# Regrouping the stages of attention, and seven by-7 steps in the second half of the down product

## The chip, the cores and the metric

The kernel runs on one core of one Trainium2 chip. The metric is the device time of one execution in microseconds (us). Before the change it is 1697.8 us, the median of three runs (1697.61 to 1697.96).

The engines are called PE (matrix products), PEld (its weight loads), DVE (vector), ACT (scalar, activations), POOL and SP (which here mostly issues DMA transfers).

## The reference

One decoder block on 256 tokens of width 2048, all in float32:

```python
a    = rmsnorm(h, norm_mix_pre)
proj = a @ w_in                      # q,k,v of 3x8 attention heads, 4 recurrence parts, 2 gates
# attention: per head three groups (window, dilation) = (128,1), (512,4), (2048,16),
#   rotary q and k, outputs mixed by their softmax denominators  -> attn (256 x 1024)
# recurrence: S_t = diag(f_t) S_{t-1} + k_t v_t^T, o_t = S_t^T q_t, per-head norm, swish gate
#   -> r_out (256 x 1024)
y = sigmoid(gate_a) * (attn @ w_attn_branch) + sigmoid(gate_r) * (r_out @ w_hgrn_branch)
h = h + rmsnorm(y @ w_mix_out, norm_mix_post)
gt, up = split(rmsnorm(h, norm_ffn_pre) @ w_ffn_gate_up)
h = h + rmsnorm((silu(gt) * up) @ w_ffn_down, norm_ffn_post)    # inner width 5632
```

The three attention groups are done as one softmax over 512 scores per query: the denominators that mix them are then those of the joint softmax.

## The kernel before

**Products.** Every large product is done in a reduced-precision format of PE with both operands split into a high and a low half (ACT rounds the high half, DVE subtracts it to get the low half). One block product is then three matmuls: high x high, high x low, low x high. Each matmul has a 128x128 stationary operand and up to 512 columns of the other. The small products of attention and recurrence, and the transposes (products with an identity matrix), are done in plain float32.

**Items.** The main loop goes over a list of items. An item is either a *chunk* of a narrow block (kind "W" and "N": 4 or 2 rows of 128 of the weight matrix) or a *step* of a wide block (256 rows, two groups of 512 columns, both halves of the tokens). A plain step is 8 block products, 24 matmuls. A *by-7* step gets the same result from 7 block products, 21 matmuls, out of sums of weight pieces and sums of activation pieces: `split_wide` makes the weight sums on DVE (lines 434, 440, 441) and splits them, and `seven_sums` (lines 522 to 529) makes and splits the activation sums. For item i the loop first calls `prepare(i)`, which splits the weights of item i+2 (tiles `w` and `wl`; for a by-7 step also `dh` and `dl`, the raw weights' halves) and starts loads further ahead. Then `multiply(i)` issues the matmuls into the PSUM banks `acc` or `aux`. Then `advance(evacs)` issues one part of a finished block's evacuation, and `advance_lanes()` advances each of the two lanes by one stage.

**Lanes.** A lane holds generators; each `yield` in one ends its stage for this item. The recurrence of four heads (`recurrence(half)`) runs in lane 0. It has six levels, three items each: products `q,kk` in the first item, DVE work on `at`, `kk`, `q` and `end` in the second, nothing in the third. A queue holds the attention of 2 x 4 heads (line 913); a free lane takes the next head. A head has two parities `par`, and each of these has the scores (3 products, `aux<-qk,qk`), the masked maximum on DVE (line 917), exponential and sum on ACT (line 921), reciprocal and scaling on DVE (lines 923, 924), four transposes on PE (line 930), their copy on ACT (line 933) and four products with the values (`aux<-pt,v`). Their items, counted from the scores, are 0, 1, 1, 2, 4, 5 and 6, and the next parity's scores are in item 7. After the second parity's values one more item writes the result's high half (ACT, line 943) and low half (DVE, line 944). So PE does something for one parity in items 0, 4 and 6.

The order in each engine's queue is the order in which this loop issues; nothing reorders it afterwards. Tiles of one tag share a fixed number of buffers: three `w` slots, so the split of item i+2 waits until PE has read the weights of item i-1; four `aux` banks; sixteen slots `r` of 128x1024 floats that hold, in the down product, the activations `act` loaded from DRAM, their halves `a`, the activation sums `so` and the gains `fpost`.

**Down product.** The last two wide blocks multiply the inner activations with `w_ffn_down`, each with 22 steps (m = 0 to 21) and 1024 output columns. `DOWN` (line 47) names the by-7 steps: 4, 7, 10, 13, 16, 19 in the first half and 3, 6, 9, 12, 15, 18 in the second. `prep_act` (line 1397) loads, splits and, for a by-7 step, sums the activations of a step; the sums of step m are kept under `a7[m]`, and so the two halves compute theirs separately. While the second half begins, DVE and ACT still evacuate the first (`down_sum` line 1425, `down_square` line 1429, `down_gain` line 1434, tile `fz`).

Of the kernel before, what the change touches and what calls it, by code (L numbers as in the profile page):

```python
# [17 lines left out]
AF = mybir.ActivationFunctionType  # L18
OP = mybir.AluOpType

P = 128
S = 256
# [3 lines left out]
KF = FF // P  # L26
# [17 lines left out]
GATE_UP3 = [(3, 0), (4, 0), (0, 2), (5, 0), (1, 1), (6, 0), (2, 2), (7, 0)]  # L44
GATE_UP4 = [(4, 0), (5, 0), (0, 2), (6, 0), (1, 1), (2, 2), (3, 1), (7, 0)]
PLACE = (0, 2, 1, 3)
DOWN = [[(m, m in by7) for m in range(KF // 2)] for by7 in (range(4, 20, 3), range(3, 19, 3))]

N_F, N_RAW, N_SPLIT, AHEAD, WARM, BRIDGE = 15, 3, 3, 2, 8, 6

# [50 lines left out]
def tile_hybrid_block(ctx: ExitStack, tc: tile.TileContext, t, out):  # L101
    nc = tc.nc
# [22 lines left out]
    def aux():  # L125
        return auxp.tile([P, 512], F32, tag="aux", name=nm("aux"))
# [7 lines left out]
    def small(s, n=8, bufs=6):  # L134
        return cpool.tile([P, n], F32, tag=f"small{n}", bufs=bufs, name=nm(s))

    def mm(ps, lhsT, rhs, start, stop):
        nc.tensor.matmul(ps, lhsT, rhs, start=start, stop=stop, skip_group_check=True)  # L138
# [66 lines left out]
    def ptile(s):  # L205
        pool, n = (wide_pool[-1], 2) if wide_pool else (fp[0], 5)
        return pool.tile([P, 512], F32, tag="p", bufs=n, name=nm(s))
# [344 lines left out]
    class Split:  # L552
# [20 lines left out]
        def high(self, n, src):  # L573
            nc.scalar.activation(self.slots[n][:, :, 0, :], src, AF.Copy)
# [84 lines left out]
    def flush(q):  # L659
        while q:  # L660
            advance(q)

    def advance_lanes():
        for lane in lanes:
            if not lane and queue:
                lane.append(queue.popleft())
            advance(lane)

    def flush_lanes():
# [201 lines left out]
    qkT, vN = {}, {}  # L871
# [28 lines left out]

    attnT, recT = [], []

    def attention(half, h):
        o = None
        for par in range(2):
            own = slice(par * P, (par + 1) * P)
            ps = aux()
            for g in range(3):
                q, k = qkT["q", half, g], qkT["k", half, g]
                if g == 0:  # L910
                    mm(ps[:, :S], q[:, h, own], k[:, h, :], True, True)
                else:
                    mm(ps[:, P * (g + 1) : P * (g + 2)], q[:, h, own], k[:, h, own], True, True)
            yield
            p = ptile("p")
            m = small("m")
            nc.vector.tensor_tensor_reduce(
                out=p, in0=ps, in1=amask[:, par, :], scale=1.0, scalar=3e38,
                op0=OP.add, op1=OP.min, accum_out=m[:, 0:1],
            )  # L920
            nc.scalar.activation(p, p, AF.Exp, scale=-1.0, bias=m[:, 0:1], accum_out=m[:, 1:2])
            yield
            nc.vector.reciprocal(m[:, 2:3], m[:, 1:2])
            nc.vector.tensor_scalar(p, p, m[:, 2:3], None, op0=OP.mult)
            yield
            yield
            ps = aux()
            for c in range(4):
                cols = slice(c * P, (c + 1) * P)
                nc.tensor.transpose(ps[:, cols], p[:, cols], ident)  # L930
            yield
            pt = ptile("pt")
            nc.scalar.activation(pt, ps, AF.Copy)
            yield
            if o is None:
                o = aux()
            for c in range(4):
                v = vN[half, max(c - 1, 0)][:, c if c < 2 else par, h * P : (h + 1) * P]
                mm(o[:, own], v, pt[:, c * P : (c + 1) * P], c == 0, c == 3)
            yield  # L940
        hi, lo, _ = attnT[0](4 * half + h)
        ov = o[:, :S].rearrange("p (two j) -> p two j", two=2)
        nc.scalar.activation(hi.rearrange("p (j two) -> p two j", two=2), ov, AF.Copy)
        nc.vector.tensor_sub(
            lo.rearrange("p (j two) -> p two j", two=2), ov,
            attnT[0].f32(4 * half + h).rearrange("p (j two) -> p two j", two=2),
        )
        yield


    def recurrence(half):
# [25 lines left out]
        def added(c):  # L977
            ps = aux()
            for n in range(2):
                mm(ps, onesr, hl[c][n], n == 0, n == 1)  # L980
            return ps
# [31 lines left out]
        for lev, w in enumerate(LEVELS):  # L1013
            rows = P - w if w > 8 else P
            ps = aux() if w > 1 else added(0)
            for e in range(8) if w > 1 else ():
                es = slice(e * P, (e + 1) * P)
                mm(
                    spans(ps[:rows, e * 64 : (e + 1) * 64], w), kk[:, e * P : e * P + rows],
                    spans(q[:, es], 2 * w)[:, :, w:], True, True,  # L1020
                )
            yield
            if w < 32:
                nc.vector.copy_predicated(
                    at[:rows].rearrange("p (e n w) -> p e n w", e=8, w=2 * w)[:, :, :, w:],
                    lmask[:rows, lev, :].rearrange("p (n w) -> p n w", w=w)[:, None, :, :]
                    .to_broadcast([rows, 8, 64 // w, w]).bitcast(I32),
                    ps[:rows].rearrange("p (e n w) -> p e n w", e=8, w=w),
                )
# [12 lines left out]
            used += n  # L1042
            nc.vector.tensor_mul(new, end[:, :, 0], end[:, :, 1])
            end = new
            if w == 8 and half == 0:
                nc.scalar.preload_act_table_set("natural_log_exp_and_others")
            yield
            yield
# [352 lines left out]
    def prep_act(m, by7):  # L1401

        q = prepared[0] // 2
        prepared[0] += 1
        fetch_act(q + (m % 2 and 2))
        f = act_in[q][:, m % 2 * 2 : m % 2 * 2 + 2, :]
        x = parts_of[m] = Split("a", 2)
        x.high(0, f)
        yield
        x.low(0, f)  # L1410
        if by7:
            dst = rslot("so").rearrange("p (z n t) -> p z n t", z=2, n=4)
            high, low = seven_sums(f, dst)
            high()
            a7[m] = sums_of(dst)
            yield
            low()
# [74 lines left out]

    def start_attention(half):
        def go():
            queue.extend(attention(half, h) for h in range(4))
        return go

    def begin_branches():
# [202 lines left out]
```

## Time and profile before

| | |
|---|---|
| median of three runs | 1697.8 us |
| the profiled execution | 1698.13 us |
| its span, first to last instruction | 1696.3 us |
| mean granted PE clock | 0.998 |
| instructions | 21711 |

In the rows that follow, `L138` is the line of the one matmul helper, so most PE rows carry it and have to be told apart by their tiles. A row of the timeline gives start, duration, engine, line, operation, result and operands, shape, count, and in brackets the idle time just ahead of it with what ended it. [...] A row of the chain of waits gives start, duration, engine, tile, line and count of the instructions merged into one piece. A row of the waits gives who waited for whom, with total, times and longest.

### The profile page before, as it was taken

What the parts mean: (1) busy time and instruction counts of PE and PEld (TensorE: products, weight loads), DVE (VectorE), ACT (ScalarE), POOL (GpSimd) and SP (SyncE); (2) the same over time, 40 slices, a digit from 0 to 9 for tenths busy, and PEclk for the clock granted to TensorE, in tenths of its full rate; (3) what the DMA queues carried; (4) which work ended last, traced back from release to release, by engine and by line L of the source; (5) the groups of instructions that cost most, each with busy time, mean ns of one, the idle gap of its engine ahead of it and who ended that gap; (6) DMA issues with size and microseconds to landing.
All of it is one profiled execution on the core that took longest, in us unless ns stands there. A gap on an engine that the chain in (4) does not pass through costs nothing.

```text
span 1696.3 us, 21711 instructions
## 1 busy us (share of the span) xinstructions
PE 1685.2 (99%) x8260; PEld 1416.7 (84%) x8260; DVE 1436.2 (85%) x1662; ACT 914.7 (54%) x1034; POOL 3.9 (0%) x13
## 2 busy tenths in 40 slices
PE   9999999999999999999999999999999999999997
PEld 7888888888888888888888888888888888888886
DVE  6999888867998988885668888888888888898997
ACT  6655555544444434445445547555555555565663
POOL 0000000000000000000000000000000000000000
PEclk9999999999999999999999999999999999999999
DMA  8667666768677767787858646777777777777773
GB/s 285 205 224 243 230 233 228 234 222 309 225 254 252 256 223 243 253 310 275 295 172 275 210 162 227 269 250 252 254 255 253 249 248 272 257 266 256 248 244 130
DMA packets 228904, 413.48 MB, mean 244 GB/s; under 512 B 12816, under 2 KB 79552, under 8 KB 226240
## 3 DMA queue, kind: packets, MB, share of 16 engines
q1 hardware_dynamic: 218544, 373.93, 65.4%
q10 hardware_dynamic: 10192, 38.15, 6.0%
q8 instruction: 64, 1.05, 0.3%
q14 instruction: 40, 0.33, 0.1%
q0 software_dynamic: 64, 0.02, 0.0%
HBM read 376.92 MB, written 35.13 MB: 243 GB/s over the span
## 4 chain that ended last, share of the span: by engine, by line
PE 98%; DVE 1%; ACT 0%; issue 0%; DVEq 0%; ACTq 0%
PE acc L138 62%; PE aux L138 34%; PE aux L930 0%; DVE wl L420 0%; PE aux L610 0%; PE aux L1348 0%; DVE fz L1475 0%; PE acc L1348 0%; ACT w L418 0%; ACT junk L1429 0%; PE aux L597 0%; DVE e L1425 0%; PE aux L1110 0%; DVE yT L578 0%; PE aux L1220 0%
## 5 line engine op out<-in xcount | busy, mean ns | idle before, releaser
L138 PE MATMUL acc<-xT,w 128*128 128x256 f32 (+1 forms) x2048 | 366.8, 338 | 0.0
L420 DVE TENSOR_TENSOR wl<-raw,w 128x2048 fp32r<-128x2048 f32 (+1 forms) x141 | 306.6, 2182 | 68.8 <-ACT w L418 67.1
L138 PEld LDWEIGHTS acc<-xT,w 128*128 128x128 f32 x2048 | 311.9, 188 | 44.7 <-DVE w L365 0.3
L418 ACT ACTIVATE w<-raw 128x2048 fp32r<-128x2048 f32 (+1 forms) x141 | 256.3, 1827 | 109.3 <-PE acc L138 35.1
L364 ACT ACTIVATE w<-raw 128x1024 fp32r<-128x1024 f32 x176 | 185.7, 1058 | 220.5 <-PE acc L138 169.6
L365 DVE TENSOR_TENSOR w<-raw,w 128x1024 fp32r<-128x1024 f32 x176 | 214.8, 1221 | 95.9 <-ACT w L364 95.2
L138 PE MATMUL acc<-w,xT 128*128 128x512 f32 x578 | 169.1, 392 | 0.0
L439 ACT ACTIVATE w<-sum 128x1024 fp32r<-128x1024 f32 x56 | 59.5, 1063 | 177.8 <-DVE sum L434 170.6
L138 PE MATMUL acc<-w,hT 128*128 128x512 f32 x472 | 152.7, 391 | 0.4 <-DVE hT L1232 0.4
L447 DVE TENSOR_TENSOR wl<-sum,w 128x1024 fp32r<-128x1024 f32 x112 | 134.8, 1221 | 13.2 <-ACT w L439 13.2
L138 PEld LDWEIGHTS acc<-w,xT 128*128 128x128 f32 x578 | 108.1, 188 | 22.2
L138 PE MATMUL aux<-w,hT 128*128 128x512 f32 x374 | 120.0, 389 | 0.0
L449 DVE TENSOR_TENSOR dl<-raw,dh 128x1536 fp32r<-128x1536 f32 x56 | 98.3, 1756 | 14.3 <-ACT dh L445 12.2
L138 PE MATMUL aux<-w,xT 128*128 128x512 f32 x344 | 109.8, 389 | 0.0
L138 PEld LDWEIGHTS acc<-w,hT 128*128 128x128 f32 x472 | 88.5, 188 | 19.0 <-DVE hT L1232 0.8
L138 PE MATMUL acc<-wl,hT 128*128 128x512 f32 x236 | 91.9, 389 | 0.0
L445 ACT ACTIVATE dh<-raw 128x1536 fp32r<-128x1536 f32 x56 | 82.7, 1476 | 8.0 <-PE aux L138 4.4
L138 PE MATMUL acc<-w,a 128*128 128x512 f32 x268 | 83.7, 389 | 0.0
L138 PE MATMUL aux<-w,a 128*128 128x512 f32 x268 | 83.7, 389 | 0.0
L138 PEld LDWEIGHTS aux<-w,hT 128*128 128x128 f32 x374 | 70.2, 188 | 14.6
L138 PE MATMUL acc<-w,so 128*128 128x512 f32 x234 | 78.8, 391 | 0.0
L138 PEld LDWEIGHTS aux<-w,xT 128*128 128x128 f32 x344 | 64.6, 188 | 13.4
(298 smaller groups left out, 2964.3 us busy)
## 6 DMA issues: line engine op xcount, KB each, us to landing
raw<-in_w_in SPq DMA_DIRECT2D x270, 512.0 KB, 4.8
raw<-in_w_ffn_gate_up SPq DMA_DIRECT2D x156, 512.0 KB, 4.8
raw<-in_w_ffn_down SPq DMA_DIRECT2D x88, 512.0 KB, 5.4
pre<-in_w_ffn_gate_up SPq DMA_DIRECT2D x40, 512.0 KB, 6.5
presum<-pre ACTq DMA_DIRECT2D x20, 1024.0 KB, 4.7
s<-presum SPq DMA_DIRECT2D x40, 512.0 KB, 7.0
raw<-in_w_mix_out SPq DMA_DIRECT2D x32, 512.0 KB, 4.9
act<-acts SPq DMA_DIRECT2D x22, 512.0 KB, 6.5
```

What stands on the lines that cost most here:

```text
L138: nc.tensor.matmul(ps, lhsT, rhs, start=start, stop=stop, skip_group_check=True)
L364: nc.scalar.activation(wh, raw, AF.Copy)
L365: nc.vector.tensor_sub(wl, raw, wh.bitcast(F32))
L418: nc.scalar.activation(hi[:, c], raw[:, c], AF.Copy)
L420: nc.vector.tensor_sub(lo[:, c], raw[:, c], hi[:, c].bitcast(F32))
L439: nc.scalar.activation(hi[:, :1024], s[:, :1024], AF.Copy)
L445: nc.scalar.activation(dhi, d, AF.Copy)
L447: nc.vector.tensor_sub(lo[:, c], s[:, c], hi[:, c].bitcast(F32))
L449: nc.vector.tensor_sub(dlo, d, dhi.bitcast(F32))
```

## The change

Two things are changed.

**Attention.** A lane now takes one generator that works through the queue of heads without leaving it. Within a parity the stages are: scores in item 0, maximum and exponential in item 1, scaling in item 2, transposes in item 3, copy in item 4, nothing in item 5, products with the values in item 6. The next parity's or next head's scores stand in that same item 6, just behind the products with the values. The result's high half is written in the next item just ahead of the maximum, its low half just behind the exponential. A generator that starts while lane 0 is busy puts its first scores off until an item in which the recurrence has issued a level's products (`beat`), three items at the most.

**Down product.** The second half has by-7 steps 2, 4, 7, 10, 13, 16 and 18, seven instead of six. Five of these (4, 7, 10, 13, 16) are by-7 steps of the first half too; their activation sums are kept from there (`m not in a7`) and not made again, which holds five of the sixteen `r` slots from one half to the other.

```diff
-DOWN = [[(m, m in by7) for m in range(KF // 2)] for by7 in (range(4, 20, 3), range(3, 19, 3))]
+DOWN = [[(m, m in by7) for m in range(KF // 2)] for by7 in (range(4, 20, 3), (2, 4, 7, 10, 13, 16, 18))]
...
+    tick, beat = [0], [0]
+
     def advance_lanes():
+        tick[0] += 1
         for lane in lanes:
             if not lane and queue:
-                lane.append(queue.popleft())
+                lane.append(attention())
             advance(lane)
...
-    def attention(half, h):
-        o = None
-        for par in range(2):
+    def attention():
+        done = []
+        for _ in range(3):
+            if not lanes[0] or tick[0] == beat[0]:
+                break
+            yield
+        while queue:
+            half, h = queue.popleft()
+            o = None
+            for par in range(2):
...
                 yield
+                for part in done[:1]:
+                    part()
                 p = ptile("p")
...
                 nc.scalar.activation(p, p, AF.Exp, scale=-1.0, bias=m[:, 0:1], accum_out=m[:, 1:2])
+                for part in done[1:]:
+                    part()
+                done = []
                 yield
...
                 nc.vector.tensor_scalar(p, p, m[:, 2:3], None, op0=OP.mult)
-            yield
-            yield
+                for _ in range(1):
+                    yield
                 ps = aux()
...
                 nc.scalar.activation(pt, ps, AF.Copy)
-            yield
+                for _ in range(2):
+                    yield
                 if o is None:
                     o = aux()
...
                     mm(o[:, own], v, pt[:, c * P : (c + 1) * P], c == 0, c == 3)
-            yield
-        hi, lo, _ = attnT[0](4 * half + h)
...
+            done = attended(4 * half + h, o)
+        yield
+        for part in done:
+            part()
+        yield
+
+    def attended(k, o):
...
+        return [high, low]
...
             ps = aux() if w > 1 else added(0)
+            beat[0] = tick[0]
...
-        if by7:
+        if by7 and m not in a7:
             dst = rslot("so").rearrange("p (z n t) -> p z n t", z=2, n=4)
...
-            queue.extend(attention(half, h) for h in range(4))
+            queue.extend((half, h) for h in range(4))
```

What the change moves is seen at three places. The first is PE's queue at the first scores of attention, which run beside the second recurrence. Before, the scores (`aux_4998`) stand by themselves between two chunks of weights:

```order
L138 MATMUL acc_4915<-xT_123,w_4908 128x256 x2
L138 MATMUL acc_4915<-xT_123,w_4908 128x512
L138 MATMUL aux_4998<-qk_3895,qk_3654 128x256
L138 MATMUL aux_4998<-qk_4372,qk_4129 128x128
L138 MATMUL aux_4998<-qk_4824,qk_4601 128x128
L138 MATMUL acc_4914<-xT_124,w_4946 128x512
L138 MATMUL acc_4914<-xT_124,w_4946 128x256 x2
```

Now they stand one chunk later, behind the products of a recurrence level (`q`, `kk`):

```order
L138 MATMUL acc_4915<-xT_125,w_4946 128x256 x2
L138 MATMUL acc_4915<-xT_125,w_4946 128x512
L138 MATMUL aux_5019<-q_3441,kk_4545 128x64 x8
L138 MATMUL aux_5028<-qk_3895,qk_3654 128x256
L138 MATMUL aux_5028<-qk_4372,qk_4129 128x128
L138 MATMUL aux_5028<-qk_4824,qk_4601 128x128
L138 MATMUL acc_5040<-xT_118,w_4974 128x512
```

The first transposes stand in both programs behind the same level's products (those of 112 rows), so from the scores to the transposes there are now three chunks where there were four. In the whole program PE's float32 products form 75 stretches between other matmuls where they formed 85; seven of the ten that are gone lay among the chunks of kind "W" and three among those of kind "N".

The second place is DVE's queue at this first softmax: `p` and `m` are its tiles, `w` the low half of a chunk's weights, `sum` a finished block, and `at`, `kk`, `q`, `end` the recurrence level. Before:

```order
L917 ISA p_5032,m_5033<-aux_4998,amask 128x512
L917 ISA m_5033 128x1
L365 TENSOR_TENSOR w_5038<-raw_4864,w_5038 128x1024
L241 TENSOR_TENSOR sum_5062<-acc_4914,sum_5062 128x256
L241 TENSOR_TENSOR sum_5062<-acc_4915,sum_5062 128x256
L1024 COPY_PREDICATED at_4546<-lmask,aux_5023 128x64x8
L1040 TENSOR_TENSOR kk_4545<-kk_4545,end_4547 128x64x8
L1040 TENSOR_TENSOR q_3441<-q_3441,end_4547 128x64x8
L1043 TENSOR_TENSOR end_4547<-end_4547 128x64
L923 RECIPROCAL m_5033<-m_5033 128x1
L924 TENSOR_SCALAR p_5032<-p_5032,m_5033 128x512
L365 TENSOR_TENSOR w_5077<-raw_4864,w_5077 128x1024
```

After:

```order
L241 TENSOR_TENSOR sum_5058<-acc_4914,sum_5058 128x256
L241 TENSOR_TENSOR sum_5058<-acc_4915,sum_5058 128x256
L1052 COPY_PREDICATED at_4546<-lmask,aux_5019 128x64x8
L1068 TENSOR_TENSOR kk_4545<-kk_4545,end_4547 128x64x8
L1068 TENSOR_TENSOR q_3441<-q_3441,end_4547 128x64x8
L1071 TENSOR_TENSOR end_4547<-end_4547 128x64
L929 ISA p_5068,m_5069<-aux_5028,amask 128x512
L929 ISA m_5069 128x1
L365 TENSOR_TENSOR w_5075<-raw_4864,w_5075 128x1024
L887 TENSOR_TENSOR w_5094<-sum_5058,tabs 64x512 x2
L938 RECIPROCAL m_5069<-m_5069 128x1
L939 TENSOR_SCALAR p_5068<-p_5068,m_5069 128x512
```

The maximum (line 929) has moved behind a chunk's weights, the block's sums and the level's four operations, and between it and the scaling (line 939) there are now the next chunk's weights and two halves of a rotary product (line 887, the old line 884).

The third place is DVE's queue at the start of the down product's second half, from the first `fz` on. Before, a by-7 step (m = 3) with its activation sums `s` and `so` follows:

```order
L1434 SCALAR_TENSOR_TENSOR fz_12781<-e_12660,r2c,fpost_11839 128x512
L434 TENSOR_TENSOR sum_12789<-raw_12674 128x1024
L440 TENSOR_TENSOR sum_12789<-raw_12674,sum_12789 128x512
L441 TENSOR_TENSOR sum_12789<-raw_12674,sum_12789 128x512
L578 TENSOR_TENSOR a_12785<-act_12625,a_12785 128x2x256
L522 SCALAR_TENSOR_TENSOR s_12797<-act_12625 128x128
L522 SCALAR_TENSOR_TENSOR s_12797<-s_12797,act_12625 128x128
L525 TENSOR_TENSOR s_12797<-act_12625 128x128
L526 TENSOR_TENSOR s_12797<-act_12625,s_12797 128x128
L447 TENSOR_TENSOR wl_12788<-sum_12789,w_12787 128x1024 x2
L529 TENSOR_TENSOR so_12796<-s_12797,so_12796 128x512
L449 TENSOR_TENSOR dl_12804<-raw_12674,dh_12803 128x1536
```

After, the by-7 step m = 2 stands ahead of the first `fz`, and these rows are from there the plain step m = 3 and the by-7 step m = 4:

```order
L1462 SCALAR_TENSOR_TENSOR fz_12799<-e_12660,r2c,fpost_11839 128x512
L578 TENSOR_TENSOR a_12803<-act_12625,a_12803 128x2x256
L420 TENSOR_TENSOR wl_12806<-raw_12674,w_12805 128x2048
L1462 SCALAR_TENSOR_TENSOR fz_12839<-e_12658,r2c,fpost_11839 128x512
L434 TENSOR_TENSOR sum_12845<-raw_12710 128x1024
L440 TENSOR_TENSOR sum_12845<-raw_12710,sum_12845 128x512
L441 TENSOR_TENSOR sum_12845<-raw_12710,sum_12845 128x512
L578 TENSOR_TENSOR a_12841<-act_12701,a_12841 128x2x256
L447 TENSOR_TENSOR wl_12844<-sum_12845,w_12843 128x1024 x2
L449 TENSOR_TENSOR dl_12853<-raw_12710,dh_12852 128x1536
```

Step m = 4 makes no activation sums, and two by-7 steps stand with one plain step between them where there were two.

More of the change, by code (lines that the diff above doesn't have):

```diff
@@ L901, in tile_hybrid_block @@
     attnT, recT = [], []
-    def attention(half, h):
-        o = None
-        for par in range(2):
[L906 to L913, printed above, removed]
-            yield
[L915 to L919, printed above, removed]
-            )
-            nc.scalar.activation(p, p, AF.Exp, scale=-1.0, bias=m[:, 0:1], accum_out=m[:, 1:2])
-            yield
-            nc.vector.reciprocal(m[:, 2:3], m[:, 1:2])
-            nc.vector.tensor_scalar(p, p, m[:, 2:3], None, op0=OP.mult)
-            yield
-            yield
[L927 to L930, printed above, removed]
-            yield
[L932 to L940, printed above, removed]
-        hi, lo, _ = attnT[0](4 * half + h)
[L942 to L948, printed above, removed]
@@ new lines, in attention @@
+    def attention():
[3 more added lines that the diff above has]
+                break
+            yield
+        while queue:
+            half, h = queue.popleft()
+            o = None
+            for par in range(2):
+                own = slice(par * P, (par + 1) * P)
+                ps = aux()
+                for g in range(3):
+                    q, k = qkT["q", half, g], qkT["k", half, g]
+                    if g == 0:
+                        mm(ps[:, :S], q[:, h, own], k[:, h, :], True, True)
+                    else:
+                        mm(ps[:, P * (g + 1) : P * (g + 2)], q[:, h, own], k[:, h, own], True, True)
+                yield
+                for part in done[:1]:
+                    part()
+                p = ptile("p")
+                m = small("m")
+                nc.vector.tensor_tensor_reduce(
+                    out=p, in0=ps, in1=amask[:, par, :], scale=1.0, scalar=3e38,
+                    op0=OP.add, op1=OP.min, accum_out=m[:, 0:1],
+                )
+                nc.scalar.activation(p, p, AF.Exp, scale=-1.0, bias=m[:, 0:1], accum_out=m[:, 1:2])
+                for part in done[1:]:
+                    part()
+                done = []
+                yield
+                nc.vector.reciprocal(m[:, 2:3], m[:, 1:2])
+                nc.vector.tensor_scalar(p, p, m[:, 2:3], None, op0=OP.mult)
+                for _ in range(1):
+                    yield
+                ps = aux()
+                for c in range(4):
+                    cols = slice(c * P, (c + 1) * P)
+                    nc.tensor.transpose(ps[:, cols], p[:, cols], ident)
+                yield
+                pt = ptile("pt")
+                nc.scalar.activation(pt, ps, AF.Copy)
+                for _ in range(2):
+                    yield
+                if o is None:
+                    o = aux()
+                for c in range(4):
+                    v = vN[half, max(c - 1, 0)][:, c if c < 2 else par, h * P : (h + 1) * P]
+                    mm(o[:, own], v, pt[:, c * P : (c + 1) * P], c == 0, c == 3)
+            done = attended(4 * half + h, o)
+        yield
+        for part in done:
+            part()
+        yield
@@ L951, in recurrence, with high, low @@
+    def attended(k, o):
+        hi, lo, _ = attnT[0](k)
+        ov = o[:, :S].rearrange("p (two j) -> p two j", two=2)
+        def high():
+            nc.scalar.activation(hi.rearrange("p (j two) -> p two j", two=2), ov, AF.Copy)
+        def low():
+            nc.vector.tensor_sub(
+                lo.rearrange("p (j two) -> p two j", two=2), ov,
+                attnT[0].f32(k).rearrange("p (j two) -> p two j", two=2),
+            )
+        return [high, low]
     def recurrence(half):
```

## The prediction

> **What bounds the kernel now.** The page comes first. Its row of busy times and its chain of work that ended last:
>
> ```profile
> PE 1685.2 (99%) x8260; PEld 1416.7 (84%) x8260; DVE 1436.2 (85%) x1662; ACT 914.7 (54%) x1034; POOL 3.9 (0%) x13
> ...
> PE 98%; DVE 1%; ACT 0%; issue 0%; DVEq 0%; ACTq 0%
> ```
>
> PE is the bound almost everywhere, and the chain of 98% hardly leaves it. What PE itself waited for, by the view of waits for that engine alone:
>
> ```profile
> PE aux L138 <- DVE warm L162: 1.2, 1, 1.2
> PE acc L138 <- DVE hT L1232: 0.4, 1, 0.4
> PE acc L138 <- DVE gate L1147: 0.2, 1, 0.2
> ```
>
> That is 1.8 us in 1696.3, and none of it in attention or in the down product. So there is no wait to win, and the change can be worth only three things: matmuls that are no longer there, time that PE loses in going from one kind of matmul to another, and new waits. PE is the one engine whose time counts; DVE (85%) counts where it comes late to PE.
>
> **One more by-7 step.** Two pieces of the chain, from the down product's first half, are together one period of three steps, two plain and one by-7:
>
> ```profile
> 1510.23 2.72 PE aux L138 x12
> 1512.95 12.92 PE acc L138 x57
> ```
>
> 12 + 57 = 69 = 24 + 24 + 21 matmuls take 15.64 us, 226.7 ns each, with no room between them. A plain step is 5.44 us and a by-7 step 4.76 us. The change makes one plain step a by-7 step, three matmuls fewer: **-0.68 us**, on PE's path. [...]
>
> **Fewer stretches of float32 products.** Ten of 85 go. What one costs beyond its own products is seen in the pieces of the chain around them:
>
> ```profile
> 346.03 83.60 PE acc L138 x480
> ...
> 669.30 5.58 PE acc L138 x32
> ...
> 837.91 10.94 PE acc L138 x48
> ```
>
> The first is 30 chunks of kind W without a break, 174.2 ns a matmul; 32 of them would be 5.57 us, and the piece that follows four transposes took 5.58: 0.01 us lost. The third is four chunks of kind N behind two pairs of scores; 48 matmuls at 226.7 ns are 10.88 us, it took 10.94: 0.06 us lost. With 0.01 for the seven stretches among W chunks and 0.06 at most, 0.02 at least, for the three among N chunks: **-0.2 us** (0.1 to 0.6, if each of the ten were worth 0.06). Attention's own products stay what they are.
>
> **The first softmax.** Here the change takes a chunk of room away, and I look for the new wait at the place where DVE has least of it. DVE's timeline from the last weights before the first softmax:
>
> ```profile
> 603.47 1.22 DVE L365 TENSOR_TENSOR w<-raw,w 128x1024 fp32r<-128x1024 f32 x1
> 604.61 0.68 DVE L917 CUSTOM_DVE_ANT_0 p<-aux,amask 128x512 f32<-128x512 f32 x1
> ...
> 607.13 1.22 DVE L365 TENSOR_TENSOR w<-raw,w 128x1024 fp32r<-128x1024 f32 x1 [1.83 <-ACT w L364]
> 608.28 0.75 DVE L241 TENSOR_TENSOR sum<-acc,sum 128x256 f32<-128x256 f32 x2
> ...
> 610.87 0.15 DVE L923 RECIPROCAL m<-m 128x1 f32<-128x1 f32 x1
> 611.07 0.49 DVE L924 TENSOR_SCALAR p<-p,m 128x512 f32<-128x512 f32 x1
> 611.47 1.22 DVE L365 TENSOR_TENSOR w<-raw,w 128x1024 fp32r<-128x1024 f32 x1
> 612.72 1.39 DVE L884 TENSOR_TENSOR w<-sum,tabs 64x512 f32<-64x512 f32 x2
> 614.13 1.23 DVE L365 TENSOR_TENSOR w<-raw,w 128x1024 fp32r<-128x1024 f32 x1
> ```
>
> ACT at the same place, the exponential and the next chunk's high half, which stands behind it in ACT's queue and holds DVE up for the 1.83 us:
>
> ```profile
> 605.34 0.72 ACT L921 ACTIVATE p<-p,m 128x512 f32<-128x512 f32 x1 [6.04 <-DVE m L917]
> ...
> 606.06 1.04 ACT L364 ACTIVATE w<-raw 128x1024 fp32r<-128x1024 f32 x1
> ```
>
> And PE's transposes that take the scaled `p`:
>
> ```profile
> 613.41 0.60 PE L930 MATMUL aux<-ident,p 128*128 128x128 f32 x4
> ```
>
> Now `p` is ready at 611.56, 1.85 us ahead. In the new order DVE comes to 604.61 as before, since it works through from far back without idling and what is ahead is the same. There it goes on with the next weights, whose high half no exponential holds up; from them to the end of the level is 610.87 - 607.13 = 3.74 us, so the maximum starts at 608.35. From the maximum to the exponential is 605.34 - 604.61 = 0.73 (609.08), to ACT's next weights 0.72 (609.80), to DVE's low half of them 607.13 - 606.06 = 1.07 (610.87). That low half costs 1.25, the rotary halves 1.41 (613.53), the reciprocal 0.20 and the scaling 0.49: `p` is ready at 614.22. PE has the same products ahead of these transposes in both programs (the scores have moved within that stretch), so it wants `p` at 613.41. **A new wait of 0.8 us.** Behind the waiting transposes stands PE's whole queue, so all of it is paid.
>
> The second softmax bounds this from below. Its scaling, and the matmul that follows the level's products, where the second transposes now stand:
>
> ```profile
> 634.88 0.49 DVE L924 TENSOR_SCALAR p<-p,m 128x512 f32<-128x512 f32 x1
> ...
> 634.91 0.62 PE L138 MATMUL acc<-xT,w 128*128 128x512 f32 x2
> ```
>
> DVE's order there is unchanged, `p` is ready at 635.37, and PE would want it at 634.91: 0.46 us late, if PE came there undelayed. With the first wait PE comes at 635.7, and nothing more is lost. So the two are worth 0.46 to 0.8 together, and up to 1.2 if DVE comes 0.4 later than I work out. From the third on DVE has more room; the last shows it. The chunks behind its scores are the piece from 837.91 above, and its second scaling is
>
> ```profile
> 843.79 0.48 DVE L924 TENSOR_SCALAR p<-p,m 128x512 f32<-128x512 f32 x1
> ```
>
> Three chunks are 8.2 us, so the transposes would come at 846.1, and `p` is ready at 844.27. The copy and the values have one chunk more between them than before, and the result's halves are written on ACT and DVE with several chunks to spare: nothing.
>
> **The start of the second half.** DVE's work there, 1570.19 being the four sums that evacuate the first half, 1576.30 to 1584.96 the by-7 step m = 3, 1585.62 a plain step:
>
> ```profile
> 1570.19 2.48 DVE L1425 TENSOR_TENSOR e<-acc,e 128x512 f32<-128x512 f32 x4
> ...
> 1576.30 1.22 DVE L434 TENSOR_TENSOR sum<-raw 128x1024 f32<-128x1024 f32 x1
> ...
> 1579.49 0.28 DVE L522 SCALAR_TENSOR_TENSOR s<-act 128x128 f32<-128x128 f32 x1
> ...
> 1580.42 2.35 DVE L447 TENSOR_TENSOR wl<-sum,w 128x1024 fp32r<-128x1024 f32 x2
> 1582.69 0.68 DVE L529 TENSOR_TENSOR so<-s,so 128x512 fp32r<-128x512 f32 x1
> 1583.29 1.75 DVE L449 TENSOR_TENSOR dl<-raw,dh 128x1536 fp32r<-128x1536 f32 x1
> 1584.96 0.74 DVE L1434 SCALAR_TENSOR_TENSOR fz<-e,r2c,fpost 128x512 f32<-128x512 f32 x1
> 1585.62 0.68 DVE L578 TENSOR_TENSOR a<-act,a 128x512 fp32r<-128x512 f32 x1
> ...
> 1588.43 0.74 DVE L1434 SCALAR_TENSOR_TENSOR fz<-e,r2c,fpost 128x512 f32<-128x512 f32 x1
> ```
>
> A by-7 step costs DVE 8.66 us, of which the activation sums are 0.93 + 0.60 = 1.53, so 7.13 without them; a plain step 2.81; an `fz` 0.66. Over the half DVE is relieved: 2 x 8.66 + 5 x 7.13 + 15 x 2.81 = 95.1 us against 6 x 8.66 + 16 x 2.81 = 96.9. But its beginning is denser. The sums end at 1572.67; then m = 2 (8.66, to 1581.33), `fz`, m = 3 (2.81), `fz`, m = 4 (7.13): its `dl` is done at 1572.67 + 8.66 + 0.66 + 2.81 + 0.66 + 7.13 = 1592.6. PE's first matmul with `dl`, now of m = 3:
>
> ```profile
> 1587.82 0.39 PE L138 MATMUL aux<-dl,a 128*128 128x512 f32 x1
> ```
>
> That of m = 4 comes one by-7 step later, 1587.82 + 4.76 = 1592.6. **A wait of 0.1 us**, between 0 and 0.7 (one more `fz` ahead); later by-7 steps are three apart and lack the 1.53, and the one at 18 has a DVE ahead of time.
>
> **Sum.** -0.68 - 0.2 + 0.8 + 0.1 = 0.0 us. The profiled execution took 1698.13 us, 1696.3 of them span; the median is 0.3 below it. Forecast: **1697.8 us**, no change. A difference of 0.2%, 3.4 us, is about the least that a measurement tells from none, and no term reaches it.
>
> **Rivals.**
>
> *DVE comes in time.* If ACT and DVE run the first softmax 0.8 us faster than I add up, the second one's 0.46 is also absorbed, and m = 4 is on time, the gains stand alone: -0.9, 1696.9 us. For it: these are sums of start-to-start distances, with their 0.1 us of handover each. Against it: DVE's idling there comes from ACT's order, which the new order keeps. Chance 0.2.
>
> *DVE falls behind in several places.* Moving the softmax work could make single weight splits late in the stretch where DVE has almost no idle time; two or three waits like the first one would be +1.6 to +2.4 more, 1699.4 to 1700.2. Against it: each wait of PE gives DVE the same time back. Chance 0.09.
>
> *Slower: every round of transposes waits.* The scores-to-transposes room is one chunk (2.8 us) shorter in all rounds, eight in the first half of the heads and four paired ones in the second. If scaling were paced by the scores, each round would wait again, 0.8 us by the first: 12 x 0.8 - 0.9 = +8.7, 1706.5 us. It is over 0.2% from six rounds on. Against it: the late rounds have 1.8 us to spare. Chance 0.03.
>
> *Slower: PE's clock falls.* The stage table, with a stretch that holds a 0.4 us wait of PE and the idle end (the number behind POOL is the granted clock):
>
> ```profile
> 1000.00:1010.00 10.00, 9.59 (x45) 7.55 (x44) 8.53 (x13) 5.70 (x8) 0.00 (x0) 1.00 0.32 107
> 1680.00:1697.00 17.00, 7.03 (x32) 5.48 (x30) 11.17 (x25) 3.44 (x10) 0.00 (x0) 0.79 0.38 123
> ```
>
> With 0.4 us idle the clock stays at 1.00; with 10 us it falls to a mean of 0.79. If 0.8 us sufficed and the same loss followed, 0.21 x 17 = 3.6 us: 1701.4. Chance 0.01. [...]
>
> *The change doesn't do what it says* in one respect that could be felt: the kept sums fill five `r` slots, and loads into the others start later. If that made one step's activations late, PE would lose some 2 to 5 us (up to one plain step, 5.44). I count it with the falling behind.
>
> **How the numbers follow.** The forecast holds 0.64, with an own range of 1697.2 (0.46 for the first wait, none at m = 4) to 1698.8 (1.2 and 0.7). The range goes from 1696.7 to 1699.4, from the first rival's 1696.9, less the scatter of 0.2 in the runs, to the mild end of the second. Faster by over 0.2% needs a gain that no row shows: 0.03. Slower by over 0.2%: 0.04 from the two slower rivals. Same: 0.93.
>
> **What would show it.** Right: PE's waits name the transposes (line 945) waiting for the scaling (line 939) once, for 0.5 to 1.2 us near 613; the down product's second half has seven pieces of 21 matmuls and its first `dl` of m = 4 starts within 0.7 us of the end of m = 3. Wrong: no such wait, or several; a chain that leaves PE in the down product; an activation load that lands after its step.

## The result and the profile after

The changed kernel takes 1700.16 us, the median of 21 runs (1699.41 to 1700.73), against 1697.8 for the kernel before in as many (1697.02 to 1698.37). The ratio is 1.0014, with a 95% interval of 1.0008 to 1.002: slower by 2.4 us, 0.14%. That is less than the 0.2% (3.4 us) from which the prediction counts a change as one, but it is clear of the scatter (the fastest of the new runs is slower than the slowest of the old), and it lies above the range that was forecast. The profiled execution took 1699.84 us, 1698.1 of them span, at a granted clock of 0.998.

PE is the bound as before. Busy times by engine, from the page of the changed kernel:

```profile
PE 1684.5 (99%) x8257; PEld 1415.5 (83%) x8257; DVE 1435.4 (85%) x1647; ACT 914.9 (54%) x1032; POOL 3.9 (0%) x13
```

Three matmuls are gone, and PE is busy 0.7 us less. What is new stands first in the view of PE's waits (who waited for whom, total, times, longest); the other three rows are those of before:

```profile
PE aux L945 <- DVE p L939: 2.4, 2, 1.3
PE aux L138 <- DVE warm L162: 1.2, 1, 1.2
PE acc L138 <- DVE hT L1260: 0.4, 1, 0.4
PE acc L138 <- DVE gate L1175: 0.2, 1, 0.2
```

The transposes wait for the scaled `p` twice, not once. PE's timeline at the two places, the first softmax and the sixth of sixteen:

```profile
611.21 1.69 PE L138 MATMUL aux<-q,kk 128*112 128x64 f32 x16
614.25 0.63 PE L945 MATMUL aux<-ident,p 128*128 128x128 f32 x4 [1.34 <-DVE p L939]
...
708.06 0.63 PE L945 MATMUL aux<-ident,p 128*128 128x128 f32 x4 [1.07 <-DVE p L939]
```

Two executions start up differently, and spans can only be compared when that is taken out. The last small product of the opening, in the profile of before and then of the changed kernel:

```profile
16.97 0.26 PE L722 MATMUL aux<-ident,rowg 48*128 48x48 f32 x1
```

```profile
16.31 0.26 PE L725 MATMUL aux<-ident,rowg 48*128 48x48 f32 x1
```

The profile of the changed kernel happens to have an opening that is shorter by 0.66 us. From this product to the end of the span it is 1681.8 against 1679.4 us: +2.4, what the medians say (+2.36). In the other runs below the same marker stands between 16.37 and 17.70; "from the marker" means this measure, and its zero is 1679.36. Each such number comes from one profiled execution, while each median is of several.

The sum of +2.4: two waits of 1.34 and 1.07, with some 0.15 us each from the end of the scaling to the start of the transposes, are +2.7; the eighth softmax is just late enough to add 0.1; the by-7 step is -0.68; the second half's beginning +0.2 (below). That leaves 0.1 for everything else, so the stretches of float32 products that were saved brought nothing that can be seen.

### The profile page after: what moved, and what is told of

The parts are those of the page before. It is cut to its first block, busy times and chain, and to the rows that moved or that the text cites. A ratio compares the mean times of both kernels' runs of the same rounds, so it can differ in the third digit from the quotient of the medians.

```text
span 1698.1 us, 21693 instructions
## 1 busy us (share of the span) xinstructions
PE 1684.5 (99%) x8257; PEld 1415.5 (83%) x8257; DVE 1435.4 (85%) x1647; ACT 914.9 (54%) x1032; POOL 3.9 (0%) x13
## 4 chain that ended last, share of the span: by engine, by line
PE 98%; DVE 1%; ACT 0%; issue 0%; DVEq 0%; ACTq 0%
PE acc L138 62%; PE aux L138 34%; PE aux L945 0%; PE aux L610 0%; PE aux L1376 0%; DVE fz L1503 0%; PE acc L1376 0%; DVE wl L420 0%; ACT junk L1457 0%; PE aux L597 0%; DVE e L1453 0%; DVE w L365 0%; ACT w L418 0%; PE aux L1138 0%; DVE w L887 0%
## 5 line engine op out<-in xcount | busy, mean ns | idle before, releaser
L138 PE MATMUL aux<-w,a 128*128 128x512 f32 x254 | 79.5, 389 | 0.0
```

## Where the two waits come from

DVE at the first softmax of the changed kernel. Lines 309 to 313 are the weight sums (`pre`, made ahead of time for by-7 steps far off), four operations of 0.69 us, one job every seven items. A row can begin before the one above it has ended (602.83 against 602.91), so what an operation costs is taken from start to start:

```profile
602.22 0.69 DVE L313 TENSOR_TENSOR pre<-pre 128x512 f32<-128x512 f32 x1
602.83 1.22 DVE L365 TENSOR_TENSOR w<-raw,w 128x1024 fp32r<-128x1024 f32 x1
604.49 1.23 DVE L365 TENSOR_TENSOR w<-raw,w 128x1024 fp32r<-128x1024 f32 x1 [0.44 <-ACT w L364]
...
608.23 0.68 DVE L929 CUSTOM_DVE_ANT_0 p<-aux,amask 128x512 f32<-128x512 f32 x1
...
610.76 1.23 DVE L365 TENSOR_TENSOR w<-raw,w 128x1024 fp32r<-128x1024 f32 x1 [1.83 <-ACT w L364]
...
613.61 0.49 DVE L939 TENSOR_SCALAR p<-p,m 128x512 f32<-128x512 f32 x1
```

And ACT, whose queue holds the store of those sums to DRAM (a DMA issue, line 316):

```profile
602.95 0.33 ACTq L316 DMA_DIRECT2D presum<-pre  x1
603.40 1.06 ACT L364 ACTIVATE w<-raw 128x1024 fp32r<-128x1024 f32 x1 [4.75 <-PE aux L138]
...
608.96 0.72 ACT L933 ACTIVATE p<-p,m 128x512 f32<-128x512 f32 x1 [3.96 <-DVE m L929]
```

The store can be issued only when the sums are done on DVE (602.91), and ACT's next high half of weights stands behind it. The row names PE as what ended ACT's 4.75 us of idling, but PE's products that it names were over at 602.99; ACT starts right behind its own DMA issue. DVE then waits 0.44 us for that half, and its level operations, the maximum and all that follows are late by as much. Further on the exponential heads ACT's queue and holds up the next high half in the same way (1.83 us).

The kernel before shows the same thing behind a later job of weight sums, with no exponential between, and there the row names the sums. ACT, then DVE:

```profile
700.94 0.33 ACTq L316 DMA_DIRECT2D presum<-pre  x1
701.39 1.06 ACT L364 ACTIVATE w<-raw 128x1024 fp32r<-128x1024 f32 x1 [4.64 <-DVE pre L313]
```

```profile
702.49 1.23 DVE L365 TENSOR_TENSOR w<-raw,w 128x1024 fp32r<-128x1024 f32 x1 [0.44 <-ACT w L364]
```

The sixth softmax is late in another way. DVE, from the weight sums to the scaling:

```profile
699.96 0.69 DVE L312 TENSOR_TENSOR pre<-pre 128x512 f32<-128x512 f32 x1
700.68 0.69 DVE L313 TENSOR_TENSOR pre<-pre 128x512 f32<-128x512 f32 x1
701.29 1.22 DVE L365 TENSOR_TENSOR w<-raw,w 128x1024 fp32r<-128x1024 f32 x1
702.42 0.68 DVE L929 CUSTOM_DVE_ANT_0 p<-aux,amask 128x512 f32<-128x512 f32 x1
...
705.43 1.22 DVE L365 TENSOR_TENSOR w<-raw,w 128x1024 fp32r<-128x1024 f32 x1 [2.31 <-ACT w L364]
...
707.42 0.49 DVE L939 TENSOR_SCALAR p<-p,m 128x512 f32<-128x512 f32 x1
```

ACT, with the exponential and the store of the sums:

```profile
703.15 0.72 ACT L933 ACTIVATE p<-p,m 128x512 f32<-128x512 f32 x1 [4.70 <-DVE m L929]
703.21 0.33 ACTq L316 DMA_DIRECT2D presum<-pre  x1
```

Its scores are on PE at 697.14; the maximum follows only at 702.42, behind two chunks' weights, two operations of a rotary product and two weight sums, and from 695.57 to there DVE has no idle time. Here the store stands behind the exponential and holds up nothing ahead of the maximum; it is DVE's own work on the sums that makes it late. In the kernel before the sixth scores came at 708.85, far behind the same job (699.50 to 700.91 are its last two sums there). A round takes six items now instead of seven, and so the rounds move against the weight sums.

The theory to test: the loss is these two waits, and their cause is a job of weight sums in the few items ahead of a maximum. The rivals: the loss lies in the down product; the regrouping itself costs time on PE; the room of three items is too short whatever DVE has in the way.

## The experiments

Medians in us, each beside the kernel before on the same chip (21 executions of the changed kernel, 5 of `sums_off_both` and of `sums_off_spread`, 7 of `no_beat`, one of `transposes_at_2`, 11 of each of the others). The last column is one execution each.

| run | median | before | ratio, 95% | from the marker |
|---|---|---|---|---|
| changed kernel | 1700.16 | 1697.8 | 1.0008 to 1.002 | +2.4 |
| down_only | 1697.66 | 1698.02 | 0.9988 to 1.0006 | -0.4 |
| attention_only | 1700.91 | 1698.02 | 1.0008 to 1.0026 | +2.9 |
| transposes_at_4 | 1698.02 | 1698.02 | 0.9991 to 1.0009 | -0.5 |
| sums_off_sixth | 1699.48 | 1698.02 | 1.0001 to 1.0018 | +1.0 |
| sums_off_first | 1699.42 | 1698.09 | 1.0 to 1.0017 | +0.9 |
| no_beat | 1702.55 | 1698.09 | 1.0016 to 1.0037 | +3.8 |
| transposes_at_2 | 1724.41 | 1698.09 | one run | +26.9 |
| sums_off_both | 1708.09 | 1698.09 | 1.0043 to 1.0071 | +10.3 |
| sums_off_spread | 1708.48 | 1698.14 | 1.0049 to 1.0074 | +10.8 |
| sums_off_mended | 1699.4 | 1697.84 | 1.0001 to 1.0019 | +3.6 |
| down_only_step1 | 1697.92 | 1698.14 | 0.9988 to 1.0006 | -0.7 |

**The two parts of the change, and the order without its waits.** `down_only` is the kernel before with the new by-7 steps and the kept sums; `attention_only` is the changed kernel with the old steps; `transposes_at_4` is the changed kernel with one item more ahead of the transposes, and one less behind the copy:

```diff
-                for _ in range(1):
+                for _ in range(2):
                     yield
                 ps = aux()
...
                 nc.scalar.activation(pt, ps, AF.Copy)
-                for _ in range(2):
+                for _ in range(1):
                     yield
```

> The kernel before with the down product's part of the change alone. Theory (the loss is PE's two waits for the scaled p in attention, 1.5 us at the first softmax and 1.2 at the sixth): 1697.1 us, the kernel before less 0.68 for the step with three matmuls fewer, and no wait in the down product above 0.1 us. Rival down product (kept sums that fill r slots, or the denser start of the second half, lose the time): 1699 us or more.

> The changed kernel with the old by-7 steps in the second half, so attention's part of the change alone. Theory: 1700.8 us, the changed kernel plus 0.68, with both waits as they were. Rival down product: 1697.8 to 1698.5.

> The changed kernel with the transposes back in item 4 and the copy in item 5; the values and the next scores stay in item 6, and the down product stays changed. Theory: both waits go, since each scaled p gets one chunk (2.8 us) more and the waits were at most 1.5; 1697.1 to 1697.4 us. Rival regrouping (PE loses time by the new order itself, whatever it waits for): 1700 us. If merging float32 stretches gains nothing, it lies at the time of the down product's change alone; if it gains the 0.2 that was forecast, up to 0.2 below it.

The rival of the down product falls: its part alone is no slower than the kernel before, and attention's part alone carries the whole loss, with the same row of waits (2.4 us, two times, 1.3 at most). In `transposes_at_4` no row of PE's waits names `p`, and the 2.7 us are back, so the regrouping by itself costs nothing. It gains nothing either: from the marker it stands at -0.5, beside the -0.4 of `down_only`, which has the old attention. The medians agree with that within their intervals, but can't tell 0.4 us apart; here the traces carry the argument. Two of the three expectations were too good: `down_only` lies at 1697.66 instead of 1697.1, with a late `dl` of 0.17 us where at most 0.1 was expected (below), and the median of `transposes_at_4`, 1698.02, is 0.6 us above its range, on a chip where the kernel before took 0.2 more.

Why fewer stretches are worth nothing is seen in the chain. One paired round of the second half of the heads in the kernel before, from the first row to the last:

```profile
814.38 10.94 PE acc L138 x48
826.19 5.46 PE acc L138 x24
833.42 2.74 PE acc L138 x12
837.91 10.94 PE acc L138 x48
```

And in the changed kernel:

```profile
810.27 3.54 PE aux L138 x28
813.81 8.22 PE acc L138 x36
822.90 8.20 PE acc L138 x36
831.11 3.54 PE aux L138 x28
```

Before, a round is 23.53 us with 84 matmuls; at 226.7 ns they are 19.04, so its three float32 stretches take 4.49. After, it is 20.84 with 72 matmuls, 16.32, and two stretches take 4.52. So in this round the extra time goes with the float32 products and not with the number of their stretches, and joining two of them saves none of it.

**The weight sums as the cause.** A counter holds the generator of the weight sums still for seven items at one place; the later jobs move with it. For `sums_off_sixth` at call 95, for `sums_off_first` at call 67:

```diff
         if fp and back and not hold[0]:
+            if turn[0] == 95 and rest[0]:
+                rest[0] -= 1
+                return
+            turn[0] += 1
             advance(back)
```

> The changed kernel with the weight sums (lines 309 to 313, four DVE operations of 0.69 us) that stand ahead of the sixth maximum put off by one period of seven items, and the later ones with them. Theory with the weight sums as the cause of the second lateness: the wait of 1.24 us at the sixth softmax goes and the one of 1.5 at the first stays, 1698.9 us. Rival (the room between scores and transposes is too short there by itself, whatever stands ahead on DVE): the second wait stays above 0.8 us, 1700.1 us.

> The changed kernel with the weight sums ahead of the first maximum put off by one period of seven items. Those ahead of the sixth maximum stay where they were. Theory with the weight sums as the cause (their four operations, and their store, which holds ACT's queue until they are done): DVE and ACT reach the first maximum about 2.9 us earlier, the scaled p is there at 611.4 for transposes at 612.7, and the first wait of 1.5 us goes while the second stays: 1698.7 us against 1700.2 of the changed kernel. Rival (the first softmax is late by the level's products and operations and the short room, not by the weight sums): the wait stays above 1 us, 1700.1 us.

Each takes away the wait it was aimed at and leaves the other. PE's waits for `p` of `sums_off_sixth`, then of `sums_off_first`:

```profile
PE aux L950 <- DVE p L944: 1.3, 1, 1.3
```

```profile
PE aux L950 <- DVE p L944: 1.1, 1, 1.1
```

The remaining 1.3 is the first softmax's, the remaining 1.1 the sixth's. The first softmax of `sums_off_first`, DVE and then PE:

```profile
605.74 0.68 DVE L934 CUSTOM_DVE_ANT_0 p<-aux,amask 128x512 f32<-128x512 f32 x1
...
608.26 1.23 DVE L369 TENSOR_TENSOR w<-raw,w 128x1024 fp32r<-128x1024 f32 x1 [1.83 <-ACT w L368]
...
611.12 0.48 DVE L944 TENSOR_SCALAR p<-p,m 128x512 f32<-128x512 f32 x1
```

```profile
611.74 1.69 PE L138 MATMUL aux<-q,kk 128*112 128x64 f32 x16
613.27 0.61 PE L950 MATMUL aux<-ident,p 128*128 128x128 f32 x4
```

The 1.83 us behind the exponential is still there, but the maximum comes 2.9 us earlier against PE, and `p` is ready at 611.60, 1.7 us ahead. From the level's products to the transposes PE takes 1.53 us here and took 3.04 in the changed kernel: the wait cost 1.5. The gains from the marker, 1.5 and 1.3, are those forecast; the medians move by 1.0 and 0.9, with intervals that hold both, and so lie 0.6 to 0.7 us above the times expected.

**The room.** `no_beat` takes out the delay of the first scores; `transposes_at_2` puts the transposes one more item earlier (no `yield` ahead of them, three behind the copy).

> The changed kernel without the delay to the recurrence's level: the first scores come one chunk earlier, where they stood in the kernel before. Theory (room against DVE's order): the first scaled p is ready as in the kernel before, 611.55 on its clock, and the transposes come one chunk and one level's products before 613.41, at 609.4: a first wait of 2.1 us in place of 1.5. The later rounds stand otherwise against the weight sums, so in total 1699.5 to 1701.5 us. Rival (the waits come from the alignment with the level's products): the first wait goes, 1698.7 us.

> The changed kernel with the transposes one item earlier still, in item 2, right behind the issue of the scaling. Theory: each round has 2.8 us less room. The rounds that had 0.15 us or waited (first, sixth, eighth) lose 2.8 each, the second 1.8, the fourth 2.3, the fifth 1.0, the four pairs 0.5 to 1.1 each: 15 us at most, 8 at least since a wait of PE gives DVE time back, so 1708 to 1716 us. Rival (waits at two special places, not a matter of room): still two or three waits, under 1704 us.

PE's waits and its first transposes in `no_beat`:

```profile
PE aux L941 <- DVE p L935: 3.8, 2, 2.3
```

```profile
611.99 0.66 PE L941 MATMUL aux<-ident,p 128*128 128x128 f32 x4 [2.35 <-DVE p L935]
```

The first wait is 2.35 us where 2.1 were expected, and the rival, that the delay causes the waits, falls: the delay made the first one shorter. A second wait, of 1.5 us at the fourth softmax, appeared that was not forecast, and the total, 1702.55, is 1 us above the range that was given. `transposes_at_2` shows what the room is worth: eight waits for `p`, 16.7 us, and three more, 1.9 us, that are put down to the reciprocal just ahead of the scaling. The rival of two or three waits falls. But the time, 1724.41 in a single execution, is above the range that was given. At the first softmax the level's products also dropped out from ahead of the transposes, which the expectation forgot, and PE waited 5.55 us instead of some 4.3; and part of the time was lost at half clock, an estimated 6.5 us (last section).

**All weight sums out of the way, with the transposes in item 3.** Three attempts: seven items at each of the two places (`sums_off_both`), the same with the wait for the loads of the last seven jobs two items shorter (`sums_off_spread`), and five items at each place with two later jobs one item shorter (`sums_off_mended`).

> The changed kernel with the weight sums off both places; the transposes stay in item 3. The last two weight sums are then done together when attention ends. Theory: no wait for p above 0.2 us, 1697.4 us, the time of the kernel with the transposes back in item 4 and of that with the down product's change alone, unless the last sums cost something at the end of attention. Rival (transposes in item 3 lose in other rounds as soon as these are mended): waits of about 1 us turn up elsewhere, 1699 us or more.

> The kernel with the weight sums off both places, and the seven last ones two items shorter each, so that they are done before attention's branch begins instead of at once there. Theory: the 6.9 us wait at the end of attention goes and no wait for p above 0.2 us comes, so the whole change without its two waits: 1697.4 us, the time of the kernel with the transposes in item 4. Rival (the denser weight sums make the paired rounds late, which have 1.5 to 2.3 us and get 1.4 us of sums between maximum and scaling): waits of 0.2 to 1 us there, 1698 to 1699.5 us.

> The changed kernel with the weight sums put off by five items ahead of the first maximum and five more ahead of the sixth, and two of the later ones one item shorter, so that none is left over when attention ends. The transposes stay in item 3. Theory (the two waits are all that attention's part costs, and their cause is the weight sums just ahead of the maximum): no wait for p above 0.2 us and 1697.4 us, what the transposes in item 4 gave. Rival (the room in item 3 is too short as soon as DVE has anything else in the way): waits of 0.5 to 2 us where the sums now fall, 1698.5 to 1700 us.

In `sums_off_both` no wait for `p` is left, as expected. But the last job was left over when the branch that takes attention's result had begun, and was done at once there. DVE waits for its load, and PE for the weights behind it; the kernel takes 10.7 us more than expected. DVE first:

```profile
872.89 0.69 DVE L309 TENSOR_TENSOR pre<-pre 128x512 f32<-128x512 f32 x1 [8.04 <-DMA pre<-in_w_ffn_gate_up]
```

```profile
877.33 0.79 PE L138 MATMUL acc<-w,attnT 128*128 128x512 f32 x1 [6.72 <-ACT w L368]
```

`sums_off_spread` ran into the same wait in the paired rounds: loads that were given two items less did not land in time (DVE idled 4.51 us for the one that it sums from 857.82 on), and PE's transposes waited 5.3 us in three waits, far more than the rival's 0.2 to 1 us. `sums_off_mended` clears the first and the sixth softmax, and its profile shows the wait at two other places, the fourth softmax (1.7 us), where the moved sums now stand ahead of the maximum, and the ninth (1.8 us), where a shortened load was late (DVE idled 4.77 us for it). DVE at the fourth, from the moved sums on:

```profile
669.86 0.69 DVE L313 TENSOR_TENSOR pre<-pre 128x512 f32<-128x512 f32 x1
...
673.98 0.68 DVE L934 CUSTOM_DVE_ANT_0 p<-aux,amask 128x512 f32<-128x512 f32 x1
```

In the changed kernel these sums stood behind this maximum, and it had 0.5 us to spare. The rival of this run is what happened: the forecast 1697.4 was not reached in any of the three. The profile of `sums_off_mended` also was the slowest of its 11 executions (1701.37 against a median of 1699.4), so the late load is probably not in all of them; no other execution shows it either way. Together these runs bear out the cause in another way: the wait goes where the weight sums go. And they put a limit on the theory: with the transposes in item 3 one such job ahead of a maximum uses up the room, and jobs that come every seven items tend to meet some round of six. Whether another placement would leave all rounds free was not shown, and no run moves the store alone out of ACT's queue, so its share of the first wait is read from the traces.

**The by-7 step's own cost.** `down_only_step1` has step 1 by-7 in the place of step 2, so that two plain steps lie ahead of step 4.

> The kernel before with the down product's change alone, and step 1 in the place of step 2, so that two plain steps lie between it and step 4. Theory (the 0.2 us that step 4's late dl takes in the kernel with the down product's change come from one plain step between 2 and 4): that 0.2 goes, 1697.2 us. Rival (step 1 is prepared while DVE still adds up the first half's last sums): its own dl or wl comes late, by 1 us or more, 1698 us or more.

The first `dl` of step 4 in the changed kernel, with the matmuls around it (0.23 us apart where nothing waits):

```profile
1594.57 0.39 PE L138 MATMUL aux<-dh,a 128*128 128x512 f32 x1
1594.86 0.50 PE L138 MATMUL aux<-dl,a 128*128 128x512 f32 x1
1595.20 0.39 PE L138 MATMUL aux<-dh,a 128*128 128x512 f32 x1
```

The distances of 0.29 and 0.34 are 0.06 and 0.11 too long: 0.17 us. With step 1 no distance there is too long, and from the marker the run stands at -0.7 where `down_only` stands at -0.4: the whole 0.68 of the step. The rival, that step 1's own weights come late, is not seen. The median, 1697.92 where 1697.2 was expected, is 0.2 below the kernel before and can't tell it from either kernel. So by their traces `down_only`, `transposes_at_4` and this run stand 0.4 to 0.7 us ahead of the kernel before, but none of them is shown to be faster: each interval holds 1.

## Why the prediction was wrong, by its own steps

- **One more by-7 step, -0.68**: right. From the marker `attention_only` stands at +2.9 and the changed kernel at +2.4. The step is worth 0.5 there, 0.68 less the 0.17 of the late `dl`, and 0.7 in `down_only_step1`, where `dl` is not late.
- **Fewer stretches, -0.2**: wrong, it is 0 within some 0.05 (`transposes_at_4` against `down_only`, and the round above). The 0.06 that a piece of the chain loses behind scores goes with the scores in the new place too (8.22 us for 36 matmuls in the changed kernel, 8.16 at 226.7 ns), and joining their stretch to another does not save it.
- **The first softmax, +0.8**: the mechanism was right, the size was 1.5. On the clock of the changed kernel's profile the opening is 0.66 earlier, for DVE as for PE: in `transposes_at_4`, whose marker stands at 17.08, `p` was ready at 614.85, against 614.10 at a marker of 16.31. Put on the clock of the prediction, the maximum came at 608.89 instead of 608.35, and `p` at 614.76 instead of 614.22. The step that failed is "the next weights, whose high half no exponential holds up": no exponential, but the store of the weight sums, in the same queue. That is the 0.44 us of idling, 0.54 with the handover. The row at 702.49 of the kernel before shows the same 0.44. Behind it every distance came out as added up, but the 0.15 us from the end of the scaling to the start of the transposes was put at nothing: 0.8 + 0.54 + 0.15 = 1.5.
- **"From the third on DVE has more room; the last shows it"**: this is where the forecast was lost, by a new wait put at nothing. The last round is a round beside chunks of kind N, without rotary work; it has its 1.5 us (transposes at 843.14, `p` ready at 841.61). The sixth lies among the W chunks of the second half of the queries and keys, 11.7 us earlier than before, behind a job of weight sums. Looking at the last round could not show it; laying the six-item rounds against the seven-item jobs could have. It cost 1.2 us. Nor is it the only round with little room: the fourth has 0.5 us, and the eighth is 0.1 late.
- **The second softmax absorbed**: right, 1.0 us to spare (`p` ready at 634.77, transposes at 635.79).
- **m = 4's `dl`, +0.1**: right, 0.17, though the prediction's own sums put the `dl` and PE's want of it at the same 1592.6.
- **The rival that came**: "DVE falls behind in several places", at +1.6 to +2.4, is what happened in kind, with two waits of like size. That its top, 1700.2, is the time measured is luck: it stood for three more waits of 0.8 us, and what came was a first wait 0.7 longer than forecast, one more of 1.2, and no gain from the stretches. It was given 0.09, on the argument that each wait gives DVE the same time back. That holds for the second softmax, right behind the first. It is no argument for one 94 us later. The range, cut at this case's mild end, ended 0.8 us below the result. (The lower end of the forecast's own range, with 0.46 and no wait at m = 4, adds up to 1697.4 and not 1697.2.)

The sum as it should have stood: -0.68 + 0 + 1.5 + 1.2 + 0.1 (the eighth) + 0.2 = +2.3, 1700.1 us.

## What to carry to other kernels

When a step of a pipeline gets a shorter room, check every round of it, not the first and the last: lay its new period against every other periodic job in the same queues, and count the DMA issues in an engine's queue as work that waits and holds up what is behind it (here a store of 0.33 us that was issued when its sums were done, and 0.44 us of idling on DVE behind it). Price a change of order by the span of a whole round less its matmuls, not by what one piece loses. And when the expected gain is a fraction of a microsecond, take out the opening of each profiled execution before two spans are compared.

## What the runs showed of the hardware

In `transposes_at_2` the granted clock falls to half three times. These stretches, and one behind a wait that left the clock alone (from 687): times, length, busy time and count of PE, PEld, DVE, ACT and POOL, and then the granted clock:

```profile
613.58:620.41 6.83, 6.09 (x21) 5.30 (x22) 3.07 (x5) 0.60 (x1) 0.00 (x0) 0.50 0.87 302
687.00:692.00 5.00, 5.00 (x32) 4.48 (x33) 3.47 (x6) 1.11 (x3) 0.00 (x0) 1.00 0.70 237
709.15:712.57 3.42, 3.42 (x14) 2.94 (x13) 3.35 (x6) 0.60 (x1) 0.00 (x0) 0.50 0.59 200
746.70:750.11 3.41, 3.41 (x12) 2.95 (x12) 0.34 (x1) 0.60 (x1) 0.00 (x0) 0.50 0.54 176
```

The first begins within the wait of 5.55 us (to 614.32); its 21 matmuls, of mixed shapes, take 0.29 busy us each, those from 687.00 on, at full clock, 0.16. The second begins 0.2 us after a wait of 1.88 us has ended (708.90). After a wait of 2.59 us (to 686.96) the clock stays at 1.00, and so it does in and after the 6 us from 636 on, in which PE idles 2.19 us. With the transposes behind the wait, PE had some 2.4 us without a large product ahead of the second stretch, and 3.0 us ahead of 687.37, where the clock did not fall. So the length of a wait alone doesn't decide here, with the transposes or without them, and what does was not shown. The half clock lasts 6.83, 3.42 and 3.41 us; in `sums_off_both` it lasts some 10.2 us, from within PE's wait of 6.72 us on (the granted clock is 0.78 from 870 to 877, 0.50 from there to 884 and 0.99 to 890). Over the whole span the granted clock is 0.994 in `transposes_at_2`, 0.995 in `sums_off_both` and 0.996 in `sums_off_spread`. PE's 12.92 busy us at half clock are an estimated 6.5 us lost, a quarter of the +26.9 of `transposes_at_2`; its waits are the 18.6 us above.

In the changed kernel itself the clock fell at neither wait: it is 1.00 from 611.0 to 614.5 and from 704.0 to 708.2, which hold the waits of 1.34 and 1.07 us, and still 1.00 from there to 620.0 and to 713.0. Over the whole span it is 0.998, before and after.
